# Small products on parts of TensorE's array, issued with the parts in turn

## The chip, the cores and the metric

The kernel runs on one core of one Trainium2 chip. The metric is device time in microseconds, the median of several runs. TensorE (PE) has two clock levels, 1.2 and 2.4 GHz; the profile gives the granted share of the full clock.

## What is computed

The reference is two blocks of a network on 256 tokens of width 2048, all in f32. The first has 16 meta tokens ahead of the sequence and mixes attention with a state space layer; the second mixes three branches, two of which are recurrences with a state of 128 x 128 for each head. What the change touches, cut from the reference:

```python
# block 1, state space: 64 groups of 16 channels, each with a complex state of 64
_, states = lax.associative_scan(_ssm_combine, (a, bu), axis=0)
y = jnp.real(jnp.einsum('lbgp,ghp->lbgh', states, c_c))          # the read-out
# block 1, attention: window of 128 plus 16 meta tokens, 16 heads of 64, 4 key heads
out = (jnp.einsum('bnkgqs,bnskd->bnqkgd', p_band, v_band)
       + jnp.einsum('bnkgqm,bmkd->bnqkgd', p_meta, v_meta))
```

In block 2 the delta rule needs the inverses of unit triangular matrices of 128 x 128 (one for each head, chunk and direction), and the gated linear attention needs the scores of pairs of tokens under products of gates, for 8 heads, 2 chunks of 128 tokens and 2 directions.

## The kernel before

**The weight stream.** `load_w` (L320) brings 128 x 1024 pieces of weights from DRAM, ACT rounds each to the high part (L328) and DVE subtracts to get the low part (L329). `linear` (L337) and `linear_t` (L373) multiply the parts with the activations' parts, three fp32r products for each pair of tiles (L349 to L351, L384 to L386). These products carry the lowest priority (`band(2)`), the loads `band(0)`, everything else `band(1)`. The order of each engine's queue is fixed when the kernel is built: a list scheduler takes, by priority, what it expects to be ready; the stream's products fill PE wherever a chain of `band(1)` waits. On the chip each engine then works its queue in that order.

**State space read-out.** `ssm_tile` (L592) handles one of 8 channel tiles with 4 state tiles. For a state tile, PE makes the input (L622), DVE rotates, scans (L630) and multiplies the state by cosines and sines into two tiles, and four f32 products of 128 rows, 32 columns and 256 moving columns add up in 32 partitions of `yps` (L635). These 32 partitions are one of four column parts of the array. After the fourth state tile DVE adds the skip term into `gel` (L636). The state and its products share one tag with five buffers (L273).

**Attention.** `attend` (L763) takes one key head and 128 queries at a time. At the end, for each half of the heads, two or three groups of tokens (16 meta tokens, 128, and for the second queries another 128) are multiplied with the probabilities; a half writes 64 of the 128 partitions of `o` (L814). The normalised keys lie in three tiles of 4 x 192 columns a token tile (`kp`, L668), written by one operation of DVE in `head_norm` (L661).

**Merge of blocks.** `merge_blocks` (L1150) puts inverses of 32 x 32 blocks together to 64 and to 128. For a pair of blocks it takes three stages (L1168, L1170, L1172), each of 8 small products into one PSUM tile and one eviction by ACT (L1174, L1176, L1178). The block pairs (`lo`, direction `d`, group of heads `g`) lie on different rows and columns of the array. It runs twice for the context (4 heads each) and once for all 8 heads.

**Scores.** In `gla_x`, for a head, a chunk and a direction, three products make the upper levels (L1497, L1504); then for each of four blocks of 32 tokens, six f32 products of 128 rows, 32 columns and 32 moving columns go to the 32 partitions of that block (L1509, L1510).

An f32 product shows in the trace as two matmul records, an fp32r product as one.

Of the kernel before, what the change touches and what calls it, by code (L numbers as in the profile page):

```python
# [53 lines left out]
def layout(inp):  # L54
# [42 lines left out]
    # block 2  # L97
# [40 lines left out]
    # constants of the shapes  # L138
# [18 lines left out]
    up = (i_[:, None] <= i_[None, :]).astype(np.float32)          # [s, t]: s <= t  # L157
# [13 lines left out]
    # segment sums [j, level, t]  # L171
# [9 lines left out]
    # transform at the 256 frequencies (f + 1/2) / 512; f and 255 - f share the sums over the even tokens (2 m)  # L181
    # and over the odd ones (2 m + 1): [m, (cos even, sin even, cos odd, sin odd), f], and the inverse [f, .., m]
# [18 lines left out]
# ----------------------------------------------------------------------------  # L201
# device side
# ----------------------------------------------------------------------------
def emit(tc, I, out, vat, cat):
# [29 lines left out]
    @contextmanager  # L234
    def behind(*ins):
        """activations of the block queue behind the given ones: the tables of their functions change once"""
        with ExitStack() as es:
            for i in ins:
                es.enter_context(tc.issue_after(i.ins))
            yield  # L240

    def dma(out_, in_):
        """transfer of a chain: ahead of the stream's"""
        with band(-1):
            nc.sync.dma_start(out_, in_)
# [27 lines left out]
    t_p = p2.enter_context(tc.tile_pool(name="t", bufs=5))  # L273
# [34 lines left out]
    side = [None, 0.0, 0.0]      # work that rides on the stream: generator, steps per load, steps due  # L308
# [11 lines left out]
    def load_w(ap):  # L320
        """ap: [128, 2048] in DRAM -> two halves of (hi, lo) parts"""
# [16 lines left out]
    def linear(xh, xl, W, ci, evict, toks=((0, 128), (128, 256)), kb0=0, nkb=None, mid=None):  # L338
        """token-major chunk of 512 columns: evict(t, psum)"""
# [12 lines left out]
        for kb in range(nkb):  # L352
            held = []
            for i, h, l in load_w(W[ci, kb0 + kb]):
                if kb < nkb - 1:
                    for t in range(len(toks)):
                        products(t, kb, i, h, l)
                else:
                    # the last weights: one token tile after the other, so that the first is evicted early
                    products(0, kb, i, h, l)  # L360
                    held.append((i, h, l))
# [11 lines left out]
    def linear_t(xh, xl, W, ci, n, evict, mid=None):  # L373
        """channel-major chunk of 256 columns (2 channel tiles) for n tokens: evict(j, psum)"""
# [18 lines left out]
    def split(src, hi, lo, scale=None):  # L393
        """hi + lo = src * scale, src in PSUM or SBUF"""
# [23 lines left out]
    def transpose_in(src, hi, lo, gcol, k, tag="a"):  # L418
        """src: list of (ap [p, D], p); one k tile into hi/lo [128, sum p]"""
# [8 lines left out]
    def ada_steps(p, row, dst, j0, n):  # L428
        """dst[:, j0 + j] = sum_k silu(c)[k] w_ada[k, (j0 + j) * 128 + p] + b_ada, for n column tiles"""
# [19 lines left out]
    def modulate_in(src, dst, sc, sh, k, ks=None):  # L449
        """k tile of the transposed src * sc + sh, split into dst"""  # L450
# [11 lines left out]
    # =====================================================================  # L462
    # block 1: norm, projections
    # =====================================================================
# [8 lines left out]
    p1.close()  # L473

# [18 lines left out]
    def poly(o, xx, coef):  # L493
        """o = sum coef[i] xx^i, highest last"""
# [5 lines left out]
    def exp_parts(a, nm_):  # L500
        """returns p2 = 2^n and q = expm1(r) with a = n ln2 + r"""
# [31 lines left out]
    # reduced angle  # L533
# [17 lines left out]
    # lambda_bar - 1 = em1 - 2 e sn^2 + 2 i e sn cs  # L551
# [21 lines left out]
    def rotation(s):  # L573
        """cosine, sine and negated sine of the state tile's angles over the tokens"""
# [16 lines left out]
    def ssm_tile(c, u):  # L591
        """u: [128 channels, L1] in SBUF; channel tile c -> gel[c]"""  # L592
# [21 lines left out]
        yps = psum("sm", [128, NT])  # L614
        for j in range(4):
            s = 4 * c + j
# [14 lines left out]
            pc, ps_ = (tl(t_p, [128, 2, L1], "t")[:, :, 0:NT] for _ in range(2))  # L631
            tt(pc, z[:, :, 16:], cos2[:, :, 16:], ALU.mult)
            tt(ps_, z[:, :, 16:], sin[:, 0:1, 16:].to_broadcast([128, 2, NT]), ALU.mult)
            for i, (pr, w) in enumerate(((pc[:, 0], Cr), (pc[:, 1], nCi), (ps_[:, 0], nCi), (ps_[:, 1], nCr))):
                T.matmul(yps[32 * j:32 * j + 32, :], w[:, j], pr, start=(i == 0), stop=(i == 3))  # L635
# [18 lines left out]
    def head_norm(ps, p, nh, dst):  # L654
        """ps [p, nh*64] -> dst [p, nh, 64] normalised (without gain)"""
# [6 lines left out]
        V.tensor_tensor(out=dst, in0=ps.rearrange("p (h d) -> p h d", d=64),  # L662
                        in1=s_[:p, :nh].unsqueeze(2).to_broadcast([p, nh, 64]), op=ALU.mult)

    kp = [tl(at_p, [128 if t < 2 else 16, 4, 192], f"kp{t}") for t in range(3)]
    vv = [tl(at_p, [128, 256], f"vv{t}") for t in range(3)]
    for t in range(3):
        nc.gpsimd.memset(kp[t], 0.0)  # L668
# [3 lines left out]
    def ev_kv(t, ps):  # L672
        p = 16 if t == 2 else 128
        head_norm(ps[:, 0:256], p, 4, kp[t][:p, :, 64:128])
# [3 lines left out]
    def turn_k():  # L678
        for v in range(4):
            for h in range(2):  # L680
                with band(0):
                    ps = psum("a", [128, L1])
                    for t, (lo, hi) in enumerate(toks3):
                        p = hi - lo
                        T.transpose(ps[:, lo:hi], kp[t][:p, v, 64 - 64 * h:192 - 64 * h], ident[:p, :p])
# [20 lines left out]
    # =====================================================================  # L706
    # block 2: modulation of the context, its state projections
    # =====================================================================
# [66 lines left out]
    def attend(v, t):  # L775
# [35 lines left out]
        for half in range(2):  # L811
            for i, (lo, hi, tv) in enumerate(groups):
                p = hi - lo
# [15 lines left out]
    def chan_norm(src, goff, gname):  # L829
        """rmsnorm over 8 channel tiles [128, NT]; into mixT[goff:]"""  # L830
# [55 lines left out]
    def turn_h(c):  # L886
        """the 4 k tiles of x's chunk c, times the gain of the norm"""
# [23 lines left out]
    def mlp(xT, Wu, Wd, evd, scale=None, mid=None, after=None):  # L911
        """evd(c, g): eviction of a chunk; scale: row [128, NT] of factors of the tokens before the activation;
        mid: work after the first half of the first product; after(c): after the last group's chunks"""
# [40 lines left out]
    grow = scratch("grow", [2, D])  # L954

    # lower bounds
# [9 lines left out]
    def gla_gates(xs, hb, nh):  # L966
        """xs: per direction (d, lf, kk, sm), tiles [128 dk, nh, NT] with the forget logits in kk:
        log forget into lf, key into kk"""
# [3 lines left out]
        for d, lf, kk, sm in xs:  # L972
# [4 lines left out]
            # the two factors of max(f, 1e-30), each in the range of Ln  # L977
# [13 lines left out]
    def excl_scan(o, g, rev, n):  # L991
        """o[t] = sum of g over j > t (rev) or j < t, over the last axis"""
# [45 lines left out]
    def conv_silu(p, o, src, r0, wname, wcol, row):  # L1038
        """o: short convolution along the tokens (rows of `row` tokens) and silu of src[r0:r0+128] (DRAM)"""
# [11 lines left out]
    def l2n(p, pk, xs, scales):  # L1051
        """each of xs [128, NT]: * scale / sqrt(sum over partitions x^2 + 1e-6), in place"""
# [17 lines left out]
    def delta_gates(p, pk, src):  # L1070
        """g, beta and exponentials of sums of g, tokens on partitions; kept in pk"""
# [8 lines left out]
        # log1p(e) = 2 atanh(e / (2 + e))  # L1080
# [20 lines left out]
        # exponentials of the sums: inclusive prefix, exclusive suffix, total; [128, kind, dir, c, h]  # L1101
# [13 lines left out]
    def block_inverse(p, MX, XT, KD):  # L1115
        """32x32 diagonal blocks of MX [128, 2 KD, 128] (unit triangular, diagonal not stored): the inverses
        go to MX, their transposes to XT [128, 2 KD, 64]"""
# [32 lines left out]
    def merge_blocks(p, MX, XT, KD):  # L1150
        pt = tl(p, [128, KD, 64], "T4c")
        for n, los in ((32, (0, 64)), (64, (0,))):
            work = [(lo, d, g) for lo in los for d in range(2) for g in range(KD // 8)]
            for stage in range(3):
                for lo, d, g in work:
                    one, two = slice(lo, lo + n), slice(lo + n, lo + 2 * n)
                    a, q = (one, two) if d == 0 else (two, one)
                    xc = slice(a.start % 64, a.start % 64 + n)
                    ks = slice(d * KD + g * 8, d * KD + g * 8 + 8)
                    # pt rows q: the block of direction d; both directions of one lo share its other half  # L1160
                    pg = pt[q, g * 8:g * 8 + 8, 0:n]
                    if stage == 2 and not (n == 32 and lo == 64 * d):
                        continue
                    ps = psum("sm" if d else "tp", [128, 8, n])
# [719 lines left out]
```

## Time and profile before

| | |
|---|---|
| runs | 3671.91, 3675.52, 3684.11 us; median 3675.52 |
| profiled execution | span 3676.8 us, from the first to the last instruction; the profile gives no other time for it |
| PE busy | 3504.3 us, 95% |
| DVE, ACT busy | 2609.8 us, 71%; 1882.7 us, 51% |
| DMA | 755.29 MB, 205 GB/s over the span |
| TensorE clock | mean granted share 0.979 |

Busy time is the time in which an engine has an instruction under way. Matmuls overlap one another, so what a product costs PE is read from the start of one record to the start of the next, not from its duration.

### The profile page before, as it was taken

The page shows a single profiled execution, that of the slowest core. Times are in us where ns is not written, and L with a number is a line of the kernel's source. Part 1 is how long each engine was busy: PE and PEld are TensorE (multiplying, and loading weights), DVE is VectorE, ACT ScalarE, POOL GpSimd, SP SyncE. Part 2 cuts the span into 40 slices and gives each one's busy share as a digit, 9 for nine tenths or more (in the row PEclk, how much of TensorE's full clock was granted, in tenths as well). Part 3 has the DMA queues.
Part 4 walks back from the last instruction along what each step waited for, and adds up shares of the span by engine and source line. Part 5 has one row for each costly group of instructions (what it writes and reads, how often), then busy time and mean ns, then how long its engine had stood idle before and what let it go on. Part 6 is the DMA issues. An engine that isn't in the chain of part 4 may idle for free.

```text
span 3676.8 us, 59387 instructions
## 1 busy us (share of the span) xinstructions
PE 3504.3 (95%) x23228; PEld 3027.8 (82%) x23228; DVE 2609.8 (71%) x4047; ACT 1882.7 (51%) x2945; POOL 2.3 (0%) x7
## 2 busy tenths in 40 slices
PE   6899999999999989989999999999999999999998
PEld 6568689887887869789888889877887798989897
DVE  8887777696968656666957578888865665555557
ACT  4466766544356434445536555645444454535353
POOL 0000000000000000000000000000000000000000
PEclk9999999999999999999989999999999999999999
DMA  8844346565667778776656864466556566666655
GB/s 290 272 160 130 118 162 191 178 205 176 212 205 250 247 246 257 244 257 220 203 181 207 291 203 149 155 202 197 166 182 196 192 216 223 212 225 217 214 191 174
DMA packets 272419, 755.29 MB, mean 205 GB/s; under 512 B 52301, under 2 KB 97525, under 8 KB 271093
## 3 DMA queue, kind: packets, MB, share of 16 engines
q1 hardware_dynamic: 272138, 751.49, 62.7%
q8 instruction: 182, 2.98, 0.3%
q14 instruction: 99, 0.81, 0.1%
HBM read 720.37 MB, written 31.01 MB: 204 GB/s over the span
## 4 chain that ended last, share of the span: by engine, by line
PE 57%; DMA 16%; DVE 10%; issue 4%; ACT 2%; SPq 0%; DVEq 0%; ACTq 0%
DMA w<-in_w_ada_dram 10%; PE ps L351 9%; PE ps L350 9%; PE ps L349 9%; PE ps L385 7%; PE ps L386 7%; PE ps L384 7%; DVE wl L329 4%; DVE w L439 1%; ACT wh L328 1%; PE ps L1509 1%; DVE T4c L488 1%; PE ps L635 1%; DMA w<-in_hy_w_dram 1%; PE ps L1170 1%
## 5 line engine op out<-in xcount | busy, mean ns | idle before, releaser
L328 ACT ACTIVATE wh<-w 128x1024 fp32r<-128x1024 f32 x1016 | 1074.1, 1058 | 1201.5 <-PE ps L351 533.1
L329 DVE TENSOR_TENSOR wl<-w,wh 128x1024 fp32r<-128x1024 f32 x1016 | 1236.6, 1220 | 577.0 <-ACT wh L328 571.7
L384 PE MATMUL ps<-Ah,wh 128*128 128x256 f32 (+1 forms) x3904 | 1116.0, 286 | 26.0 <-DVE r L491 16.4
L386 PE MATMUL ps<-Ah,wl 128*128 128x256 f32 (+1 forms) x3904 | 1119.4, 287 | 17.1 <-DVE wl L329 16.7
L385 PE MATMUL ps<-Al,wh 128*128 128x256 f32 (+1 forms) x3904 | 1118.4, 287 | 2.6 <-DVE Al L397 1.5
L384 PEld LDWEIGHTS ps<-Ah,wh 128*128 128x128 f32 x3904 | 747.3, 191 | 39.9 <-DVE r L491 20.0
L386 PEld LDWEIGHTS ps<-Ah,wl 128*128 128x128 f32 x3904 | 747.6, 192 | 32.3 <-DVE wl L329 22.7
L385 PEld LDWEIGHTS ps<-Al,wh 128*128 128x128 f32 x3904 | 744.0, 191 | 11.6 <-issue 6.8
L350 PE MATMUL ps<-wl,Bh 128*128 128x512 f32 x1344 | 534.4, 398 | 18.9 <-DVE wl L329 18.8
L351 PE MATMUL ps<-wh,Bl 128*128 128x512 f32 x1344 | 538.6, 401 | 0.0
L349 PE MATMUL ps<-wh,Bh 128*128 128x512 f32 x1344 | 534.4, 398 | 3.4 <-DVE r L491 2.3
L439 DVE SCALAR_TENSOR_TENSOR w<-w,cb 128x1024 f32<-128x1024 f32 x256 | 311.9, 1222 | 251.1 <-DMA w<-in_w_ada_dram 245.2
L350 PEld LDWEIGHTS ps<-wl,Bh 128*128 128x128 f32 x1344 | 254.9, 190 | 84.7 <-DVE wl L329 26.8
L349 PE MATMUL ps<-wh,Ah 128*128 128x512 f32 x752 | 298.6, 401 | 8.7 <-ACT wh L328 4.7
L350 PE MATMUL ps<-wl,Ah 128*128 128x512 f32 x752 | 302.6, 402 | 4.4 <-DVE wl L329 4.3
L349 PEld LDWEIGHTS ps<-wh,Bh 128*128 128x128 f32 x1344 | 255.5, 190 | 59.9 <-DVE r L491 3.6
L351 PE MATMUL ps<-wh,Al 128*128 128x512 f32 x752 | 300.2, 399 | 0.0
L351 PEld LDWEIGHTS ps<-wh,Bl 128*128 128x128 f32 x1344 | 254.7, 190 | 55.2 <-issue 1.4
L349 PEld LDWEIGHTS ps<-wh,Ah 128*128 128x128 f32 x752 | 139.9, 187 | 47.0 <-ACT wh L328 8.3
L350 PEld LDWEIGHTS ps<-wl,Ah 128*128 128x128 f32 x752 | 140.6, 187 | 41.6 <-DVE wl L329 7.9
L351 PEld LDWEIGHTS ps<-wh,Al 128*128 128x128 f32 x752 | 140.6, 187 | 34.9 <-issue 3.7
L923 ACT ACTIVATE r<-r 128x256 f32<-128x256 f32 x128 | 53.1, 417 | 92.0 <-DVE r L491 90.0
(566 smaller groups left out, 3424.9 us busy)
## 6 DMA issues: line engine op xcount, KB each, us to landing
w<-in_w_ff_dram SPq DMA_DIRECT2D x288, 512.0 KB, 4.7
w<-in_w_ada_dram SPq DMA_DIRECT2D x256, 512.0 KB, 4.8
w<-in_w_up_dram SPq DMA_DIRECT2D x128, 512.0 KB, 4.9
w<-in_w_down_dram SPq DMA_DIRECT2D x128, 512.0 KB, 4.9
w<-in_w_gate_dram SPq DMA_DIRECT2D x96, 512.0 KB, 4.5
w<-in_w_out_dram SPq DMA_DIRECT2D x64, 512.0 KB, 4.3
w<-in_w_hy_dram SPq DMA_DIRECT2D x48, 512.0 KB, 5.1
w<-in_w_br_dram SPq DMA_DIRECT2D x48, 512.0 KB, 4.6
```

Source lines behind the costliest of these rows:

```text
L328: A.activation(out=h, in_=w, func=AF.Copy)
L329: V.tensor_tensor(out=l, in0=w, in1=h.bitcast(F32), op=ALU.subtract)
L349: T.matmul(acc[t], xh[k][:, lo:hi], hs, start=(k == 0), stop=False)
L350: T.matmul(acc[t], xh[k][:, lo:hi], ls, start=False, stop=False)
L351: T.matmul(acc[t], xl[k][:, lo:hi], hs, start=False, stop=(k == nk - 1))
L384: T.matmul(acc[c], h[:, s], xh[k][:, 0:n], start=(k == 0), stop=False)
L385: T.matmul(acc[c], h[:, s], xl[k][:, 0:n], start=False, stop=False)
L386: T.matmul(acc[c], l[:, s], xh[k][:, 0:n], start=False, stop=(k == nk - 1))
L439: V.scalar_tensor_tensor(out=w, in0=w, scalar=1.0, in1=cb, op0=ALU.mult, op1=ALU.mult, accum_out=part[:, j, i:i + 1])
L488: V.tensor_tensor(out=o, in0=a, in1=b, op=op)
L635: T.matmul(yps[32 * j:32 * j + 32, :], w[:, j], pr, start=(i == 0), stop=(i == 3))
L923: A.activation(out=r, in_=r, func=AF.Square)
```

## The change

In four places the loops are turned so that neighbouring products in PE's queue use different parts of the array. Comments are gone as well.

1. `ssm_tile`: the four read-out products of a state tile are kept in a list; after every second state tile the products of both are issued, one of the first, one of the second, and so on. The products have tiles of their own (six buffers of 2 x 256 columns); the state keeps three. Both pools are opened after the first phase's tiles are given back.
2. `attend`: the loop over groups of tokens is now outside, the loop over halves inside.
3. `merge_blocks`: in a stage and a group of heads, all block pairs get their PSUM tile first; then product 0 of each, product 1 of each, up to 7; then their evictions.
4. `gla_x`: the six kinds of products are the outer loop, the four blocks the inner.

To make room for the buffers of 1, the keys move into eight tiles of the pool of activations; the key norm writes them by four operations of DVE, and they are cleared by nine instructions on GpSimd in place of three.

```diff
-    t_p = p2.enter_context(tc.tile_pool(name="t", bufs=5))
...
     p1.close()
+    t_p = p2.enter_context(tc.tile_pool(name="t", bufs=3))
+    pr_p = p2.enter_context(tc.tile_pool(name="pr", bufs=6))
...
         yps = psum("sm", [128, NT])
+        terms = []
         for j in range(4):
+            terms.append([])
...
-            pc, ps_ = (tl(t_p, [128, 2, L1], "t")[:, :, 0:NT] for _ in range(2))
+            pc, ps_ = (tl(pr_p, [128, 2, NT], "pr") for _ in range(2))
             tt(pc, z[:, :, 16:], cos2[:, :, 16:], ALU.mult)
             tt(ps_, z[:, :, 16:], sin[:, 0:1, 16:].to_broadcast([128, 2, NT]), ALU.mult)
             for i, (pr, w) in enumerate(((pc[:, 0], Cr), (pc[:, 1], nCi), (ps_[:, 0], nCi), (ps_[:, 1], nCr))):
-                T.matmul(yps[32 * j:32 * j + 32, :], w[:, j], pr, start=(i == 0), stop=(i == 3))
+                terms[-1].append((w[:, j], pr))
+            if j % 2:
+                for i in range(4):
+                    for jj in (j - 1, j):
+                        w, pr = terms[jj][i]
+                        T.matmul(yps[32 * jj:32 * jj + 32, :], w, pr, start=(i == 0), stop=(i == 3))
...
-        V.tensor_tensor(out=dst, in0=ps.rearrange("p (h d) -> p h d", d=64),
-                        in1=s_[:p, :nh].unsqueeze(2).to_broadcast([p, nh, 64]), op=ALU.mult)
+        if isinstance(dst, list):
+            for h in range(nh):
+                V.tensor_scalar(out=dst[h], in0=ps[:, h * 64:(h + 1) * 64], scalar1=s_[:p, h:h + 1], scalar2=None,
+                                op0=ALU.mult)
+        else:
+            V.tensor_tensor(out=dst, in0=ps.rearrange("p (h d) -> p h d", d=64),
+                            in1=s_[:p, :nh].unsqueeze(2).to_broadcast([p, nh, 64]), op=ALU.mult)
...
-    kp = [tl(at_p, [128 if t < 2 else 16, 4, 192], f"kp{t}") for t in range(3)]
+    kp = [[tl(act_p, [128, 192], f"Bh{8 + 4 * t + v}") for v in range(4)] for t in range(2)]
+    kp_m = tl(at_p, [16, 4, 192], "kp2")
+    kp.append([kp_m[:, v] for v in range(4)])
...
-        for half in range(2):
-            for i, (lo, hi, tv) in enumerate(groups):
-                p = hi - lo
+        for i, (lo, hi, tv) in enumerate(groups):
+            p = hi - lo
+            for half in range(2):
                 T.matmul(o[64 * half:64 * half + 64], vv[tv][:p, v * 64:(v + 1) * 64],
                          pts[i][:p, half::2], start=(i == 0), stop=(i == len(groups) - 1))
...
-            work = [(lo, d, g) for lo in los for d in range(2) for g in range(KD // 8)]
             for stage in range(3):
-                for lo, d, g in work:
+                for g in range(KD // 8):
+                    work = []
+                    for lo in los:
+                        for d in range(2):
+                            if stage == 2 and not (n == 32 and lo == 64 * d):
+                                continue
...
+                            work.append((a, q, xc, ks, pt[q, g * 8:g * 8 + 8, 0:n],
+                                         psum("sm" if d else "tp", [128, 8, n])))
                     for i in range(8):
-                        k = ks.start + i
+                        for a, q, xc, ks, pg, ps in work:
+                            k = ks.start + i
+                            if stage == 0:
+                                T.matmul(ps[q, i], MX[a, k, q], XT[a, k, xc], start=True, stop=True)
+                            elif stage == 1:
+                                T.matmul(ps[a, i], pg[:, i], MX[q, k, q], start=True, stop=True)
+                            else:
+                                T.matmul(ps[q, i], MX[q, k, q], pg[:, i], start=True, stop=True)
+                    for a, q, xc, ks, pg, ps in work:
...
-                    for b in range(4):
-                        s_ = slice(32 * b, 32 * b + 32)
-                        g_ = slice(t * 128 + 32 * b, t * 128 + 32 * b + 32)
-                        for i in range(5):
-                            T.matmul(cf[s_, i * 32:(i + 1) * 32], E[:, 2 + i, s_], qE[:, 2 + i, s_], start=True, stop=True)
-                        T.matmul(cf[s_, 160:192], kk[:, g_], q[:, g_], start=True, stop=True)
+                    for i in range(6):
+                        for b in range(4):
+                            s_ = slice(32 * b, 32 * b + 32)
+                            g_ = slice(t * 128 + 32 * b, t * 128 + 32 * b + 32)
+                            l_, r_ = (E[:, 2 + i, s_], qE[:, 2 + i, s_]) if i < 5 else (kk[:, g_], q[:, g_])
+                            T.matmul(cf[s_, i * 32:(i + 1) * 32], l_, r_, start=True, stop=True)
```

## Rows read from the trace of the kernel before

**Rows 1.** Cores view (span, granted clock) and page part 1: busy us, share, instructions.

```profile
core 0: 3676.8 us, clock 0.979
...
PE 3504.3 (95%) x23228; PEld 3027.8 (82%) x23228; DVE 2609.8 (71%) x4047; ACT 1882.7 (51%) x2945; POOL 2.3 (0%) x7
```

**Rows 2.** Page part 4: the chain that ended last, by engine.

```profile
PE 57%; DMA 16%; DVE 10%; issue 4%; ACT 2%; SPq 0%; DVEq 0%; ACTq 0%
```

**Rows 3.** Windows: length, busy us of each engine, granted clock, DMA share, GB/s.

```profile
200.00:530.00 330.00, 323.27 (x1847) 239.41 (x1848) 255.93 (x443) 230.59 (x450) 0.00 (x0) 0.98 0.41 134
1902.40:1926.30 23.90, 23.45 (x286) 22.25 (x283) 3.01 (x5) 9.79 (x21) 0.00 (x0) 0.50 0.35 126
2149.30:2351.80 202.50, 201.84 (x2788) 184.52 (x2786) 172.47 (x348) 115.63 (x324) 0.00 (x0) 1.00 0.44 143
```

**Rows 4.** Waits of DVE and ACT, 200 to 530: total us, times, longest.

```profile
DVE wl L329 <- ACT wh L328: 29.6, 27, 2.2
DVE g L491 <- PE ps L635: 12.9, 7, 4.3
...
ACT wh L328 <- PE ps L385: 36.7, 23, 3.1
```

**Rows 5.** Timeline of PE, a read-out: start, us, what, records.

```profile
317.77 1.05 PE L635 MATMUL ps<-t,nC 128*32 128x256 f32 x4
318.75 0.39 PE L384 MATMUL ps<-Ah,wh 128*128 128x256 f32 x1
```

**Rows 6.** Timeline of PE, two calls of attention's last products.

```profile
306.99 0.64 PE L814 MATMUL ps<-pt,vv 16*64 16x256 f32 x2
307.56 0.38 PE L384 MATMUL ps<-Ah,wh 128*128 128x256 f32 x1
307.87 1.79 PE L814 MATMUL ps<-pt,vv 128*64 128x256 f32 x6
309.59 0.50 PE L782 MATMUL ps<-Bl,Bh 128*128 128x272 f32 x1
...
350.80 3.23 PE L814 MATMUL ps<-pt,vv 16*64 16x256 f32 x12
353.96 0.50 PE L622 MATMUL ps<-Bl,lB 128*128 128x272 f32 x1
```

**Rows 7.** Timeline of PE, two merges; ACT's evictions of the second (lines view).

```profile
839.55 0.59 PE L1168 MATMUL ps<-XT,MX 32*32 32x32 f32 x13
...
852.28 1.22 PE L349 MATMUL ps<-wh,Bh 128*128 128x512 f32 x2
...
1896.73 1.19 PE L1168 MATMUL ps<-XT,MX 32*32 32x32 f32 x32
1897.88 2.34 PE L1170 MATMUL ps<-MX,T4c 32*32 32x32 f32 x64
...
1922.04 0.79 PE L1260 MATMUL ps<-T4a,Bh 128*128 128x256 f32 x1
...
L1174 ACT ACTIVATE T4c<-ps 32x256 f32<-32x256 f32 (+1 forms) x12 | 5.2, 444 | 12.9 <-PE ps L1168 12.6
```

**Rows 8.** Timeline of PE, one block of scores and what follows.

```profile
2155.99 0.33 PE L1497 MATMUL ps<-qE,E 128*64 128x64 f32 x2
...
2156.32 0.48 PE L1509 MATMUL ps<-qE,E 128*32 128x32 f32 x11
2156.60 0.20 PE L1510 MATMUL ps<-g,Bh 128*32 128x32 f32 x1
2156.63 0.20 PE L1509 MATMUL ps<-qE,E 128*32 128x32 f32 x1
2156.64 0.20 PE L1510 MATMUL ps<-g,Bh 128*32 128x32 f32 x1
2156.66 0.41 PE L1509 MATMUL ps<-qE,E 128*32 128x32 f32 x9
...
2157.60 0.49 PE L1522 MATMUL ps<-S,qP 128*128 128x128 f32 x2
```

**Rows 9.** Lines of DVE, 200 to 530: busy, mean ns.

```profile
L488 DVE TENSOR_TENSOR bt<-bcw,si 128x128 f32<-128x128 f32 x12 | 3.4, 286 | 0.2
```

More of the change, by code (lines that the diff above doesn't have):

```diff
@@ L661, in head_norm @@
         rstd_of(s_[:p, :nh], 64, 1e-6, p)
-        V.tensor_tensor(out=dst, in0=ps.rearrange("p (h d) -> p h d", d=64),
-                        in1=s_[:p, :nh].unsqueeze(2).to_broadcast([p, nh, 64]), op=ALU.mult)
-    kp = [tl(at_p, [128 if t < 2 else 16, 4, 192], f"kp{t}") for t in range(3)]
+        if isinstance(dst, list):
[8 more added lines that the diff above has]
+    kp.append([kp_m[:, v] for v in range(4)])
     vv = [tl(at_p, [128, 256], f"vv{t}") for t in range(3)]
-    for t in range(3):
-        nc.gpsimd.memset(kp[t], 0.0)
+    for k_ in (*kp[0], *kp[1], kp_m):
+        nc.gpsimd.memset(k_, 0.0)
     toks3 = ((16, 144), (144, 272), (0, 16))
@@ L673, in ev_kv @@
         p = 16 if t == 2 else 128
-        head_norm(ps[:, 0:256], p, 4, kp[t][:p, :, 64:128])
+        head_norm(ps[:, 0:256], p, 4, [k_[:p, 64:128] for k_ in kp[t]])
         A.activation(out=vv[t][:p], in_=ps[:, 256:512], func=AF.Copy)
@@ L684, in turn_k @@
                         p = hi - lo
-                        T.transpose(ps[:, lo:hi], kp[t][:p, v, 64 - 64 * h:192 - 64 * h], ident[:p, :p])
+                        T.transpose(ps[:, lo:hi], kp[t][v][:p, 64 - 64 * h:192 - 64 * h], ident[:p, :p])
                     A.activation(out=kT[v][h], in_=ps, func=AF.Copy)
@@ L1152, in merge_blocks @@
         for n, los in ((32, (0, 64)), (64, (0,))):
-            work = [(lo, d, g) for lo in los for d in range(2) for g in range(KD // 8)]
             for stage in range(3):
-                for lo, d, g in work:
[L1156 to L1164, printed above, removed]
-                    for i in range(8):
-                        k = ks.start + i
+                for g in range(KD // 8):
[4 more added lines that the diff above has]
+                                continue
+                            one, two = slice(lo, lo + n), slice(lo + n, lo + 2 * n)
+                            a, q = (one, two) if d == 0 else (two, one)
+                            xc = slice(a.start % 64, a.start % 64 + n)
+                            ks = slice(d * KD + g * 8, d * KD + g * 8 + 8)
+                            work.append((a, q, xc, ks, pt[q, g * 8:g * 8 + 8, 0:n],
+                                         psum("sm" if d else "tp", [128, 8, n])))
+                    for i in range(8):
+                        for a, q, xc, ks, pg, ps in work:
[7 more added lines that the diff above has]
+                    for a, q, xc, ks, pg, ps in work:
@@ L1167, in merge_blocks @@
                         if stage == 0:
-                            T.matmul(ps[q, i], MX[a, k, q], XT[a, k, xc], start=True, stop=True)
+                            A.activation(out=pg, in_=ps[q], func=AF.Copy)
                         elif stage == 1:
-                            T.matmul(ps[a, i], pg[:, i], MX[q, k, q], start=True, stop=True)
+                            A.activation(out=MX[a, ks, q], in_=ps[a], func=AF.Copy, scale=-1.0)
                         else:
-                            T.matmul(ps[q, i], MX[q, k, q], pg[:, i], start=True, stop=True)
@@ L1173, in merge_blocks @@
-                    if stage == 0:
-                        A.activation(out=pg, in_=ps[q], func=AF.Copy)
-                    elif stage == 1:
-                        A.activation(out=MX[a, ks, q], in_=ps[a], func=AF.Copy, scale=-1.0)
-                    else:
-                        A.activation(out=XT[q, ks, xc], in_=ps[q], func=AF.Copy, scale=-1.0)
+                            A.activation(out=XT[q, ks, xc], in_=ps[q], func=AF.Copy, scale=-1.0)
     def delta_heads(p, pk, src, h0, nh, gates, row, S_in, S_out, tb):
```

## Prediction

> **What bounds the kernel now.** I read the busy shares first: the span is 3676.8 us at a mean granted clock of 0.979, and PE is busy 95% of it [rows 1]. A busy PE can still be a waiting PE, so the chain of waits comes next: 57% of it is PE, 16% DMA, 10% DVE [rows 2]. Then the stretches where the edited products run [rows 3]. From 200 to 530 us (read-out and attention) PE is busy 323.3 of 330 us, DVE 255.9. From 1902.4 to 1926.3 (the longest merge of blocks and what follows it) PE is busy 23.5 of 23.9 us at a granted clock of 0.50, DVE 3.0. From 2149.3 to 2351.8 (scores of the gated linear attention) PE is busy 201.8 of 202.5 us, DVE 172.5. All three are PE stretches. The waits say the same: in the first, DVE's longest waits are for ACT's copy of the weights, 29.6 us, and for the read-out products, 12.9 us, and ACT's own longest wait is for PE to let go of weight buffers, 36.7 us [rows 4]. So a microsecond taken from PE's queue there is a microsecond of the kernel, until DVE fills up. The sum is made against the span of the profiled execution; it lies 1.3 us above the median of the runs (3675.52), which I neglect.
>
> **How a part-array product shows.** Each f32 product leaves two matmul records. Records on the same part follow each other; records on different parts can run side by side. The last products of one 32-column part and the first of the next show it: L1510 at 2156.60 and .64, L1509 at .63 and .66 [rows 8], so each keeps a step of 0.03 to 0.04 us while the other does too, 15 to 20 ns a record, while 32 records on one part take from 1896.73 to 1897.88, 36 ns each [rows 7]. So two parts in turn cost half. Whether four parts cost a quarter, and whether the same holds for 256 moving columns, no row shows.
>
> **(a) State space read-out (L635).** 8 channel tiles of 4 state tiles have 4 products each: 128 products, 256 records. They come in groups of two products: 4 records from 317.77 to the next other start at 318.75, 0.98 us [rows 5]. 64 groups of 0.98 are 63 us, all but a few in PE-bound time. In the new order two state tiles alternate. Their products add into one PSUM tile, and products into one PSUM tile stay in program order: at 306.99 the first half's 16-row product is followed by a product of the stream, not by the second half's 16-row product, which needed nothing more [rows 6]. So I expect the pair in three pieces: the first product of tile j-1 alone as soon as its cosine product is there (two records, 0.57 us as at 306.99 to 307.56 [rows 6]); then (j), (j-1), (j), (j-1) when tile j has its first term: four records on each of two parts, 0.98; then the last three, again at most 0.98. 2.53 us against 4 x 0.98 = 3.92, 1.4 us for each of 16 pairs: 22 us. If the halves come as two full alternating groups it is 3.92 - 1.96, 31 us; if 256-column records of two parts don't overlap it is nothing. I take 22, since the overlap at 32 columns is the nearest row. The last tile's DVE add (the 12.9 us wait) follows the last product in either order.
>
> **(b) Attention times values (L814).** With two groups of tokens it takes 306.99 to 307.56 and 307.87 to 309.59, 2.29 us; with three, 350.80 to 353.96, 3.16 us [rows 6]; four calls of each, 21.8 us. The two halves write 64 columns each and now alternate product by product: half, 10.9 us; at the other end nothing. I take 10.
>
> **(c) Merge of blocks (L1168 to L1172).** 896 records. The largest merge, 416 records without a break, lasts from 1896.73 to 1922.04, 25.3 us, and most of it at the low clock of 1.2 GHz [rows 3, 7]; one context half has 208 records in 839.55 to 852.28, 12.7 us [rows 7]; with the other half and the pieces ahead the sum is 51 us. The new loop issues up to four chains in turn. But each has a PSUM tile of its own, so order is set by when each is ready: at 1896.73 32 records of one chain run by themselves because the others' blocks have not landed, and from stage to stage each chain waits for its own eviction on ACT, 0.44 us each, 12 of them in the largest merge [rows 7]. So I count two chains at a time for half of the products: a quarter of 51, 13 us, plus 2 us for less time at the low clock. Ends: all four chains abreast and full clock, 36 us; or lockstep, PE standing behind four evictions of 0.44 us at each of 20 stages (five in each of the two context halves, and five for both groups of heads of the last merge), 35 us, less 15 to 20 regained: a loss of 15 to 20. Stream products usually fill such holes, so I take +15.
>
> **(d) Scores (L1509, now one loop).** 32 blocks (8 heads, 2 steps, 2 directions) of 1.61 us, 2155.99 to 2157.60 [rows 8]. The 48 records from 2156.32 on take 1.28 us, 27 ns each. With the four column parts in turn at the step seen for two, 16 ns, 0.77: 0.51 us a block, 16 us. Four truly abreast would be 0.36, 29 us; no overlap beyond today's, nothing. I take 16.
> The Trainium skill weighs against (d): "TensorE: Matmul & The Clock Gate", in its section on the gap of 56 ns, puts a floor of some 25 ns between starts of matmuls however few their columns. The trace has 15 to 20 over four records [rows 8], and the row decides; by the page 48 records would take 1.2 us and (d) would give 3 us.
>
> **(e) Costs added.** The key norm on DVE becomes four operations of 64 columns where there was one, three times; with a 128-column operation at 0.29 us [rows 9] that is at most 12 x 0.29 less the 3 it replaces, no shorter, 2.6 us, ahead of the queries' projection whose accumulators wait for it; at the other end it is hidden. I take 2. Nine clears on POOL instead of three have no predecessor and lie under the first projection. The buffers for the state (3 of z and its partner, 6 of the products) suffice for a pair: four products are held, two are free for the next tile, and DVE works through one tile at a time. The keys now lie in buffers that attention's outputs reuse much later. No DMA is added or moved.
>
> **Sum.** 22 + 10 + 15 + 16 - 2 = 61. What comes next as a bound is DVE in 200 to 530: it needs 255.9 of then 298 us, 86%, and in the scores 172.5 of 186, 93%. Serial chains rarely run that full, so I give back 2 us of the first and 4 of the second. 55 us net: 3676.8 - 55 = 3622.
>
> **Rivals.**
> 1. DVE takes over. With (a) and (b) worth 40% and (d) 45% of their sizes: 13 + 7 + 15 - 2 = 33 us, 3644. For it: DVE's 85% in the scores [rows 3]. Against: its waits there and in the read-out end with PE [rows 4].
> 2. More overlap: (a) 31, (b) 11, (c) 25, (d) 27, less 2 and the same 6: 86, 3591. For it: nothing in the rows caps overlap at two. Against: four abreast isn't seen.
> 3. The change doesn't do what it says: parts that share their rows do not run side by side with 256 columns, so (a) and (b) give nothing and (d) little: 15 + 3 - 2 = 16, 3661. Against it: the four starts within 0.06 us are column parts of the same 128 rows [rows 8]. For it: they are short.
> A rule of the skill says so more strictly: "TensorE: Matmul & The Clock Gate", Part 3, The mechanism, lets a weight load overlap products under way only where the row groups differ. The trace disagrees for 32 columns by the same rows.
> 4. Slower: the clock. In the merge PE was busy throughout and the granted clock still was 0.50 [rows 3]; the scores kept 1.00 with 52 of 202 us in small products. If their blocks, shortened and followed by waits for DVE, bring the clock down, each microsecond at 1.2 GHz costs half a microsecond of full-clock work. It decides from 110 us at the low clock, where the 55 are gone; if half of the scores' 186 us of work ran at the low level it would take 93 us more, 3715. Against it: the stream's full-array products still fill every gap there.
>
> **How the numbers follow.** Forecast 0.50 (own range 3607 to 3634), rival 1 0.17, rival 2 0.14, rival 3 0.11, rival 4 0.08. From 3580 to 3656 leaves out rivals 3 and 4 and little of rival 2: 0.8. A measurement of this kernel can tell 0.3%, 11 us, from no change: faster takes the forecast, rivals 1 and 2 and half of rival 3, 0.86; within 0.3% half of rival 3, 0.06; slower 0.08.
>
> **What would show it.** (a) right: read-out records of two parts starting a few ns apart and some 0.12 us a record; wrong: 0.25 us a record as now. (b) 1.1 to 1.6 us a call. (c) the merge from 1896 under 18 us; if lockstep, PE waits for ACT's evictions of L1174 to L1178. (d) blocks of 1.0 to 1.1 us; with four abreast 0.7. PE's busy total should fall by 45 to 75 us. The prediction is wrong if PE's total falls so far and the span does not: then waits for DVE in 200 to 530 or 2149 to 2350 take its place; or if the clock's mean falls below 0.979.

## The result, and the profile after

The changed kernel takes 3630.26 us (median of 4 runs, 3624.57 to 3634.63), the kernel before beside it 3677.26 (4 runs): ratio 0.986, 95% interval 0.9841 to 0.9878, which is 45 to 58 us less (the medians lie 47 us apart; the ratio on record is not their quotient, which would be 0.987). The forecast was 3622, with a range of its own from 3607 to 3634. The profiled execution has a span of 3632.9 us, 44 less than that of before; the rows below are from it.

Cores and busy shares, then the chain that ended last, of the changed kernel:

```profile
core 0: 3632.9 us, clock 0.978
...
PE 3452.0 (95%) x23228; PEld 2990.6 (82%) x23228; DVE 2610.2 (72%) x4056; ACT 1873.9 (52%) x2938; POOL 2.6 (0%) x13
...
PE 54%; DMA 15%; DVE 8%; issue 5%; ACT 3%; SPq 0%; DVEq 0%; ACTq 0%
```

PE does the same 23228 matmul records in 52 us less; DVE has what it had [rows 1]. The chain is still PE's by more than half, a little less than before [rows 2].

Windows of the changed kernel (length, busy time of each engine with instructions, granted clock, DMA share, GB/s): read-out and attention, the largest merge with its two stretches, the scores.

```profile
200.00:503.00 303.00, 294.95 (x1874) 231.41 (x1872) 256.66 (x444) 219.82 (x434) 0.00 (x0) 0.99 0.45 147
1877.03:1882.83 5.80, 5.08 (x145) 4.57 (x144) 0.00 (x0) 2.99 (x8) 0.00 (x0) 0.97 0.91 201
1882.83:1899.95 17.12, 17.12 (x290) 16.87 (x288) 1.23 (x2) 7.44 (x17) 0.00 (x0) 0.51 0.50 189
2129.50:2319.60 190.10, 185.55 (x2814) 165.31 (x2814) 174.83 (x354) 119.83 (x334) 0.00 (x0) 1.00 0.51 159
```

The first stretch has DVE's 256 us of before in 27 us less. The merge's longer part is still at 0.51 with PE busy all of it. In the scores PE, which had no idle time worth naming [rows 3], now has 4.6 us of it, and DVE stands at 174.8 of 190.1.

Waits of DVE and ACT, 200 to 503 (in all, times, longest):

```profile
DVE wl L328 <- ACT wh L327: 15.9, 20, 1.9
DVE g L492 <- PE ps L644: 11.1, 6, 2.5
...
ACT wh L327 <- PE ps L384: 27.0, 20, 2.8
```

ACT waits 27.0 us for PE where it waited 36.7 [rows 4]: PE lets go of the weight buffers sooner.

Timeline of PE, a pair of state tiles, and the early single product of another:

```profile
288.82 0.40 PE L644 MATMUL ps<-pr,bcw 128*32 128x256 f32 x1 [0.43 <-DVE pr L489]
288.83 0.40 PE L644 MATMUL ps<-pr,nC 128*32 128x256 f32 x1
289.06 0.38 PE L644 MATMUL ps<-pr,bcw 128*32 128x256 f32 x1
289.07 0.81 PE L644 MATMUL ps<-pr,nC 128*32 128x256 f32 x5
289.81 0.39 PE L385 MATMUL ps<-Ah,wl 128*128 128x256 f32 x1
...
291.53 1.05 PE L644 MATMUL ps<-pr,nC 128*32 128x256 f32 x6
292.51 0.38 PE L383 MATMUL ps<-Ah,wh 128*128 128x256 f32 x1
...
306.70 0.62 PE L644 MATMUL ps<-pr,bcw 128*32 128x256 f32 x2
307.25 0.72 PE L798 MATMUL ps<-Bl,Bh 128*128 128x272 f32 x2
```

Two parts start 10 ns apart, and eight records take the 0.99 us that four took [rows 5]. Timeline of PE, attention times values with two and with three groups of tokens:

```profile
304.88 1.23 PE L830 MATMUL ps<-pt,vv 16*64 16x256 f32 x8
306.04 0.72 PE L798 MATMUL ps<-Bl,Bh 128*128 128x272 f32 x2
...
345.33 1.66 PE L830 MATMUL ps<-pt,vv 16*64 16x256 f32 x12
346.92 1.19 PE L625 MATMUL ps<-Bl,lB 128*128 128x272 f32 x4
```

1.16 and 1.59 us for 2.29 and 3.16 [rows 6]. Timeline of PE, the long runs of the largest merge:

```profile
1877.03 1.75 PE L1188 MATMUL ps<-XT,MX 32*32 32x32 f32 x45
...
1882.83 6.02 PE L1188 MATMUL ps<-XT,MX 64*64 64x64 f32 x92
...
1893.22 3.56 PE L1188 MATMUL ps<-XT,MX 64*64 64x64 f32 x31
...
1896.64 3.38 PE L1190 MATMUL ps<-MX,T4c 64*64 64x64 f32 x63
1899.95 0.70 PE L1281 MATMUL ps<-T4a,Bh 128*128 128x256 f32 x2
```

From 1877.03 to 1899.95 there are 22.9 us where there were 25.3 [rows 7]. The first run has 35 ns a record (1877.03 to 1878.59 for 45), as one chain had before: the chains still come one after another. The row of 92 holds 32 records of 64 rows and 60 of 32 rows, and only its end alternates. Of the 64-row runs only the last, 63 records in 3.3 us, shows two parts in turn: 53 ns a record for 105 in the run of 31 ahead of it. Timeline of PE, a block of scores:

```profile
2142.16 0.33 PE L1518 MATMUL ps<-qE,E 128*64 128x64 f32 x2 [0.68 <-DVE S L492]
2142.42 0.22 PE L1525 MATMUL ps<-qE,E 128*32 128x32 f32 x2
2142.44 0.23 PE L1531 MATMUL ps<-qE,E 128*32 128x32 f32 x2
2142.47 0.20 PE L1525 MATMUL ps<-qE,E 128*32 128x32 f32 x2
2142.49 0.46 PE L1531 MATMUL ps<-qE,E 128*32 128x32 f32 x30
2143.01 0.49 PE L1544 MATMUL ps<-Bl,at 128*128 128x128 f32 x2
2143.43 0.27 PE L1531 MATMUL ps<-qE,E 128*32 128x32 f32 x8
2143.51 0.25 PE L1531 MATMUL ps<-g,Bh 128*32 128x32 f32 x8
2143.69 0.49 PE L1543 MATMUL ps<-S,qP 128*128 128x128 f32 x2
```

Eight records from 2143.43 to 2143.51, 10 ns each, where the long loop of before had 27 [rows 8].

**Where the time came from.** For the lines of each edited place (in the scores with the upper levels, which stand among them) I add up, over the timeline, the time from a block's first record to the next start of another line (us of PE, before and after): read-out 66.1 and 40.6, values 22.1 and 11.3, merges 50.9 and 49.4, scores 52.6 and 28.7: 61.7 less. Of it the span has 44 in this pair of executions. By the starts of the same products in both traces, 25.9 us are gained when attention ends (528.9 and 503.0) and 28.9 when the first merge begins (836.2 and 807.3). The stretch of the scores up to the last product behind them is 14.7 shorter (204.8 and 190.1); from the first score product to the last it is 19.4 shorter (202.4 and 183.0), and the rest lies behind them, where PE stands 2.05 us idle for ACT and works through more of the stream. Against that the dense stage from the second merge to the third, where behind that merge no line is edited, took 883.6 us at a clock of 0.97; before, 874.0 at 0.98. Single executions differ there by that much: the four kernels with one part each took 882.0 to 886.8 us (values alone, scores alone) or 873.8 to 875.0 (read-out alone, merges alone), and behind the second merge PE's queue holds the same 5239 records in the same order in all six. The lower clock level was granted for 54.6 us of the stage in the changed kernel and for 37.5 before; at half the speed the difference is worth an estimated 8.5 us, most of the 9.6. That is why parts are weighed below by their own stretches and by medians, not by the difference of two spans.

### The profile page after: what moved, and what is told of

The parts are those of the page before. It is cut to its first block, busy times and chain, and to the rows that moved or that the text cites. A ratio compares the mean times of both kernels' runs of the same rounds, so it can differ in the third digit from the quotient of the medians.

```text
span 3632.9 us, 59413 instructions
## 1 busy us (share of the span) xinstructions
PE 3452.0 (95%) x23228; PEld 2990.6 (82%) x23228; DVE 2610.2 (72%) x4056; ACT 1873.9 (52%) x2938; POOL 2.6 (0%) x13
## 4 chain that ended last, share of the span: by engine, by line
PE 54%; DMA 15%; DVE 8%; issue 5%; ACT 3%; SPq 0%; DVEq 0%; ACTq 0%
DMA w<-in_w_ada_dram 10%; PE ps L350 9%; PE ps L349 9%; PE ps L348 9%; PE ps L383 6%; PE ps L384 6%; PE ps L385 6%; DVE wl L328 4%; ACT wh L327 1%; DVE T4c L489 1%; DVE w L438 1%; PE ps L1188 1%; DVE T4a L1151 1%; PE ps L1190 0%; DMA w<-in_w_hi_dram 0%
## 5 line engine op out<-in xcount | busy, mean ns | idle before, releaser
L383 PE MATMUL ps<-Ah,wh 128*128 128x256 f32 (+1 forms) x3904 | 1117.9, 287 | 31.3 <-DVE r L492 19.4
L349 PE MATMUL ps<-wl,Bh 128*128 128x512 f32 x1344 | 536.0, 399 | 17.1 <-DVE wl L328 17.0
L350 PEld LDWEIGHTS ps<-wh,Bl 128*128 128x128 f32 x1344 | 255.1, 190 | 54.3 <-issue 1.0
L348 PEld LDWEIGHTS ps<-wh,Ah 128*128 128x128 f32 x752 | 140.6, 188 | 46.2 <-ACT wh L327 11.9
```

Source lines behind the costliest of these rows:

```text
L348: T.matmul(acc[t], xh[k][:, lo:hi], hs, start=(k == 0), stop=False)
L349: T.matmul(acc[t], xh[k][:, lo:hi], ls, start=False, stop=False)
L350: T.matmul(acc[t], xl[k][:, lo:hi], hs, start=False, stop=(k == nk - 1))
L383: T.matmul(acc[c], h[:, s], xh[k][:, 0:n], start=(k == 0), stop=False)
```

## The experiments

Theory A: in all four places PE sets the pace, so the time follows the PE time taken away. Rivals: another engine eats part of it; and for the merges, that order can't help at all.

**Each part alone, in the kernel before.** Four kernels, timed together (before 3682.28, 23 runs). The first holds the pairs of state tiles, with the buffers that they need and so the keys' normalisation; the others have one loop each in the new order.

```
 # read-out alone
...
-                T.matmul(yps[32 * j:32 * j + 32, :], w[:, j], pr, start=(i == 0), stop=(i == 3))
+            if j % 2:
+                for i in range(4):
+                    for jj in (j - 1, j):
...
 # values alone
-        for half in range(2):
-            for i, (lo, hi, tv) in enumerate(groups):
+        for i, (lo, hi, tv) in enumerate(groups):
+            for half in range(2):
...
 # merges alone
...
+                    for i in range(8):
+                        for a, q, xc, ks, pg, ps in work:
...
 # scores alone
-                    for b in range(4):
+                    for i in range(6):
+                        for b in range(4):
...
```

> The kernel before with the read-out in pairs alone (its buffers and the keys' new place with it); attention, merge and scores as before. Theory A (what an edit takes from TensorE's time comes off the span): the read-out's records fell from 66 to 41 us of TensorE time, so 25 us less, 2 of them given back by the key norm: 23 us off, about 3653. Rival (VectorE fills up in this stage): not more than 15 us off, with VectorE's waits for TensorE gone from 200 to 500 us.

> The kernel before with only attention's last products in turn. Theory A: 22.1 to 11.3 us of TensorE time, so 11 us off, about 3666. Rival (hidden beside VectorE's chain): at most 4 us off.

> The kernel before with only the merge of blocks in turn. Theory A (the chains are ready one after another, so the queue still holds them one after another): 1 to 2 us of TensorE time, no difference in the time, -4 to +2 us. Rival (lockstep: TensorE stands behind four evictions at each stage): 10 us slower or more. Second rival (the products do alternate and the gain is lost elsewhere): matmul starts in the merges half as far apart as before.

> The kernel before with only the scores in turn. Theory A: 52.6 to 28.7 us of TensorE time, 24 us off, about 3653. Rival (VectorE is at 92% in this stage and takes over): 10 to 15 us off and the stage from the first to the last score shrinks by no more than that.

Measured: read-out 3660.81, ratio 0.9938 (0.9918 to 0.9958), 21.5 us less; values 3671.48, 0.9970 (0.9957 to 0.9982), 10.8 less; merges 3679.64, 0.9988 (0.9975 to 1.0), 2.6 less; scores 3662.88, 0.9942 (0.9924 to 0.996), 19.4 less. They add up to 54.3, inside the whole change's 45 to 58, so no loss from one part to another shows within these intervals. Read-out and values come out as Theory A says. The 2.6 of the merges are not clear of no change; they speak against lockstep, which would be 10 us slower. The new buffers of the read-out were not run without the new order; its PE time in this kernel is 40 us for 66. Scores alone, the window of the stretch:

```profile
2161.60:2347.40 185.80, 183.50 (x2804) 162.78 (x2804) 173.47 (x353) 118.18 (x334) 0.00 (x0) 1.00 0.50 156
```

185.8 us for 204.8: 19.0 of the 23.9 us of PE come off, with DVE at 93% of what is left, so the rival with 10 to 15 is wrong for this stretch. The merge alone has the same long runs as in the whole change:

```profile
1906.23 6.02 PE L1172 MATMUL ps<-XT,MX 64*64 64x64 f32 x92
```

**The later tile first.** The changed kernel with one line altered.

```
-                    for jj in (j - 1, j):
+                    for jj in (j, j - 1):
```

> The changed kernel, with one thing altered: within a pair of state tiles the later tile's product comes first in each turn, so no product of the earlier tile is issued alone while the later one is still being made. Theory A (the core's time follows the TensorE time in the state-space stage): each pair is now one block of eight records, 0.98 to 0.99 us, in place of a single product of 0.55 us, eight records and a last run of six; with three single products of 0.55 us saved in part per channel tile I expect TensorE's read-out time of the stage to go from 40.6 to about 32 us, and the time 6 to 10 us below the changed kernel's, ratio to the kernel before about 0.983. Rival: the early single products fill time in which TensorE waits for VectorE's products anyway, so the later start gives all of it back; then the time is within 3 us of the changed kernel's, or 2 to 5 us above it.

Measured: 3616.35, ratio to before 0.9824 (0.9808 to 0.984); the changed kernel in the same session 3622.04, 0.9842 (0.9821 to 0.9864). The single product is gone: 18 blocks of eight records at 0.99 us and 7 of sixteen (six at 1.85, one at 2.38), 31.3 us of PE for 39.8. The medians are 5.7 us apart, but the intervals overlap: that the planner keeps the order of products into one PSUM tile is confirmed, its worth in time isn't settled.

**All four tiles at once.**

```
-            if j % 2:
+            if j == 3:
-                    for jj in (j - 1, j):
+                    for jj in (3, 2, 1, 0):
```

with 8 buffers for products in place of 6 and 2 for the state and its partner in place of 3 (the expectation calls them the exponentials').

> The changed kernel, with the read-out once for all four state tiles of a channel tile, their four column parts in turn, the last tile first; two more buffers for the products, one fewer for the exponentials. If four parts of 256 columns run beside one another as two do, a channel tile's read-out is two blocks of 16 records at about 1.0 us each, 2.0 us in place of 4.7 to 5.0 us: TensorE's read-out time falls by about 22 us, and the time by 15 to 22 us under the changed kernel's, if TensorE sets the stage. If only two parts fit, 16 records take about 2 us, the read-out stays near 32 us, and the time is like that of the kernel with the later tile first. Rival: VectorE, 257 us busy in this stage of some 300 us, now has its products held until the fourth tile, and TensorE waits for it; then the gain in TensorE time doesn't come off the span, and the time is the changed kernel's or up to 10 us longer.

Measured: 3611.14, 0.9816 (0.9794 to 0.9838); 10.9 us under the changed kernel's median. Timeline of PE in this kernel, a whole channel tile:

```profile
284.90 0.64 PE L644 MATMUL ps<-pr,bcw 128*32 128x256 f32 x8 [0.60 <-DVE pr L489]
285.36 1.48 PE L644 MATMUL ps<-pr,nC 128*32 128x256 f32 x24
286.77 0.39 PE L384 MATMUL ps<-Al,wh 128*128 128x256 f32 x1
```

32 records in 1.87 us, 58 ns each, against 245 for one part [rows 5]: four parts of 256 columns run beside one another. PE's read-out time is 16.0 us, 23.8 less than the changed kernel's, but only some 11 come off. Waits of DVE in this kernel, 88 to 530:

```profile
...
DVE t L489 <- PE ps L625: 11.9, 4, 3.7
...
DVE sBre L489 <- DMA bcw<-in_ssm_bc_dram: 7.0, 5, 2.0
DVE g L492 <- PE ps L644: 3.6, 4, 1.4
```

The wait for the read-out (the last row) is 3.6 us where the changed kernel in the same session has 11.0, and the chain of DVE's next channel tile now waits for its input product and for a transfer: 11.9 and 7.0 us, where that kernel has 5.8 and no row of 1.2 us or more for the transfer. The windows of 88 to 563 us of this kernel and of that one:

```profile
88.00:563.00 475.00, 437.36 (x2873) 360.13 (x2872) 410.23 (x714) 332.43 (x622) 0.00 (x0) 0.97 0.57 187
88.00:563.00 475.00, 448.09 (x2761) 350.41 (x2762) 400.45 (x693) 315.31 (x600) 0.00 (x0) 0.99 0.55 182
```

PE idles 37.6 us of it for 26.9, so 10.7 of the 23.8 us came back as idle time. So here the rival is half right: PE alone no longer sets the end of the stage, and DVE's serial chain takes part; which of its waits costs how much was not tested.

**Merges in forced order.** Each merge product is made to follow the one that the loop writes before it, and the block pairs are taken in reverse.

```
-                        for a, q, xc, ks, pg, ps in work:
+                        for a, q, xc, ks, pg, ps in reversed(work):
...
+                            with behind(*([] if prev is None else [prev])):
+                                    prev = T.matmul(...)
```

> The changed kernel, with the merge products of the blocks of triangular inverses chained one behind the other in the order in which the loop writes them, so that chains of different parts alternate product by product and none is issued as soon as its own inputs are ready. If the order in which chains became ready is why the merge took 49.4 us of TensorE in place of 50.9, this order makes neighbouring products use different parts, and the merge's TensorE time falls to 25 to 35 us. Of that up to 15 us come off the span, less what each stage of merges waits for all four evictions before it starts. Rival: the wait for the slowest chain at each level costs as much as the alternation saves, about 12 levels of 1 us: then the TensorE time falls, and the time is within 5 us of the changed kernel's or above it. Second rival: the products alternate and still take 32 ns each; then the parts of this shape don't run side by side at all.

Measured: 3619.37, 0.983 (0.9812 to 0.9849), 2.7 us under the changed kernel. Timeline of PE in this kernel, in the largest merge:

```profile
1861.20 1.02 PE L1190 MATMUL ps<-XT,MX 32*32 32x32 f32 x66 [3.11 <-DMA XT<-invt]
...
1865.60 1.85 PE L1192 MATMUL ps<-MX,T4c 32*32 32x32 f32 x64 [0.77 <-ACT T4c L1197]
...
1881.11 2.65 PE L1190 MATMUL ps<-XT,MX 64*64 64x64 f32 x64
1883.60 0.29 PE L1192 MATMUL ps<-MX,T4c 64*64 64x64 f32 x2
```

66 records within 1.02 us, where the changed kernel has 45 in 1.56: the parts do run side by side, so the second rival is wrong, and the order was what held them. The windows of the merge and of its last levels here:

```profile
1861.20:1886.51 25.31, 18.86 (x468) 15.97 (x468) 6.05 (x7) 14.13 (x30) 0.00 (x0) 0.60 0.67 241
1881.11:1886.51 5.40, 5.32 (x130) 4.83 (x129) 0.00 (x0) 3.47 (x7) 0.00 (x0) 0.88 0.51 167
```

PE's merge time over the kernel is 37.2 us for 52.4 in the changed kernel of the same session (49.4 in its first profile). But from the record ahead of each block to the block 14.4 us pass in all, where 2.7 passed (2.4 in the first), 8.0 of them with PE idle, and inside the 37.2 PE idles another 6.5: it waits for blocks that have not landed (the 3.11 in the first row) and for evictions on ACT. Most of the gain became waits; the first rival holds.

**Forced order for 64-row blocks alone.** By shape the forced order had taken the 64-row products from 22.5 to 10.8 us, and left the 32-row ones, with their waits, at 26.3 for 26.9. Part of the first fall is the clock: in the largest merge these levels ran at 0.51 in the changed kernel and at 0.88 here (the windows above).

```
-                        for a, q, xc, ks, pg, ps in work:
+                        for a, q, xc, ks, pg, ps in (work if n == 32 else reversed(work)):
...
+                            with behind(*([] if prev is None or n == 32 else [prev])):
...
```

> The changed kernel, with the product-by-product order forced for the merges of 64-row blocks alone; those of 32-row blocks stay as the scheduler issues them. With all merges forced, the 64-row products fell from 23 to 11 us of TensorE (two chains) while the 32-row products stayed near 26 us and TensorE waited 14 us at entries. If that reading holds, this kernel keeps the 11 to 12 us of the 64-row products and loses almost none of the waits: merge TensorE time about 38 us with entries near 3 us, and the time 5 to 12 us below the changed kernel's. Rival: what TensorE gains in the merge it waits for later, since the next consumers need the last eviction of a level; then the time is within 3 us of the changed kernel's.

Measured beside the changed kernel again (3629.52, ratio 0.9835, 0.9817 to 0.9853): 3628.33, 0.9835 (0.9816 to 0.9854). The PE time fell as expected, 41.2 us for 52.2, with 3.7 in front of blocks for 2.7; the time did not move, so the rival holds. Of where it goes I know only a part. When the third merge begins this kernel is 2.7 us ahead of the changed one; from there on PE idles 3.6 us more up to the scores and 3.7 more in the convolution branch, but the planner also put other products into these stretches (89 and 36 records), so I can't tell what of it the forced order causes. This stays open.

**Four tiles with forced 64-row blocks.** Both edits together.

> Read-out after all four state tiles together with the forced order in the merges of 64-row blocks. If both gains come off TensorE's time independently: 11 us (measured for the four tiles beside the changed kernel) plus 5 to 12 us, so 3599 to 3608 us, ratio to the kernel before 0.977 to 0.980. Rival: only the four tiles count, 3611 us, ratio 0.981.

Measured: 3619.79, 0.9808 (0.9783 to 0.9832): the rival's 0.981. It is 9.7 us under the changed kernel of its session, as the four tiles alone were 10.9 under theirs. The kernel with four tiles is the quickest seen, together with this one.

**The changed kernel again**, for the two comparisons above.

> The changed kernel unaltered, beside the other three for comparison in the same session: 3630 us, ratio to the kernel before 0.986. If the mean clock of the untouched dense stage differs from that of its first profile, that stage's length differs by 8 to 13 us with no edit.

> The changed kernel unaltered, beside the other two: 3622 to 3630 us, ratio to the kernel before 0.984 to 0.986.

Its ratios, 0.9842 and 0.9835, lie about 0.002 under the first; the three intervals overlap. From the three ratios the change is worth 51, 58 and 61 us, from the medians 47, 59 and 58. The first of the two came out 8 us below what I expected, the second within it. The dense stage took 883.9 and 880.6 us, so the 8 to 13 that I held possible did not show between profiles of the changed kernel.

## Why the prediction was right, and which term was wrong

The forecast was a net of 55 us; the parts alone give 54.3, and the whole 47 to 59 by medians. The bound was right, but the sum is right in part by luck, because errors cancel: of 63 us of PE in (a) to (d), (c) was 13.5 too high, (d) 7.9, (a) 3.5 and (b) 0.8 too low, which makes the measured 61.7.

**What bounds it.** Right. Read-out and values together took 36.3 us less of PE, and their kernels gained 32.3; the scores took 23.9 less and gained 19.4. The give-back is 4.0 and 4.5 us, against the 2 and 4 that I allowed; in the scores of the whole change it shows as PE idle, 0.7 us before [rows 3] and 4.6 after.

**(a) Read-out, 22.** Measured 25.5 of PE and 21.5 of time. The pieces came out as forecast: 0.55, 0.99 and 0.98, 2.54 us a pair (40.6 over 16) for 2.53. The base was 66.1 where I counted 63. What I left open, whether 256 columns on two parts overlap, is answered by the starts at 288.82 and .83.

**(b) Values, 10.** 10.8 of both.

**(c) Merges, 15: the step that failed.** "I count two chains at a time for half of the products" was to give 13. The changed kernel has 1.5 us less of PE, and alone the edit gives 2.6 of time, with an interval that reaches no change; the merge took 22.9 us, not under 18. Single executions spread by more than the 1.5: PE's merge time is 50.9 to 54.7 us in the four kernels with the old loop and 49.4 to 52.4 in six with the new one, 2.1 apart in the mean. I had named the reason myself, that each chain has its own PSUM tile and goes when it is ready, and should have followed it to the end: the loop writes an order, the planner issues by readiness, and one chain's eight products are ready together. The runs of 45 and 92 records show it, and the forced order shows that nothing else kept the parts from alternating. The "2 us for less time at the low clock" did not fail with it: at the largest merge the stretch at the lower level is 23.9 us long before [rows 3] and 17.1 after. In the four kernels with the old loop it is 23.9 to 27.3, in the six with the new one 17.1 to 20.5. At half the clock 6.8 us less of it are worth an estimated 3.4, so this alone could be what the merges gained. The 12 evictions that I counted for the largest merge are those of its first stage; with 16 records a chain its 448 records make 28 chains, and as many evictions.

**(d) Scores, 16: too small.** 23.9 us of PE. It is nearer to four parts abreast, the end that I had at 29: 10 ns between starts, not the 16 that I took from two parts. A block takes 0.90 us (28.7 over 32), between the 1.0 to 1.1 forecast and the 0.7 for four abreast. The Trainium skill, "TensorE: Matmul & The Clock Gate", section "Wait — 56ns, not 53.3ns?", puts a floor of about 25 ns under the distance of two starts; by this trace it does not hold between parts of the array (eight records from 2143.43 to 2143.51, 10 ns each).

**(e) Key norm, 2.** Not seen apart. One operation of 64 columns took 0.27 us, nearly as much as one of 128 with 0.29 [rows 9]:

```profile
L673 DVE TENSOR_SCALAR Bh<-ps,hss x8: 262/270/278, 154.5 to 157.7; 128x64 f32<-128x64 f32 x8
```

**Rivals.** DVE did not take over in the change itself; it does so in part in the kernel with four tiles, which takes another 24 us of PE. More overlap was true of (d), not of (c). Parts that share their rows do run side by side at 256 columns. The Trainium skill, "TensorEngine Tiling (Array Packing)", section "Available Configurations", lists four parts of 128 rows by 32 columns; the trace agrees, with the 32 records of four such parts in 1.87 us. The clock stayed at 1.00 in the scores. One sign of being wrong came up all the same: the mean clock of the profiled execution is 0.978, below the 0.979 that I set. Executions of the kernel before lie between 0.975 and 0.981, so this sign was finer than the spread and tells nothing.

## What to carry to other kernels

Products on different parts of the array overlap only if they stand next to each other in the queue; a loop that alternates them does this where they are ready together or share one PSUM tile, and a planner that goes by readiness undoes it otherwise, so look at the starts in the trace, not at the loop. Forcing the order moved most of the cost into waits, and neither forced kernel was clearly faster than the changed one; where all inputs are there at once it could pay, which was not tested. Before the sum, ask of each term whether what it needs is ready at once.

## What the runs showed of the hardware

Four column parts of 256 f32 columns run abreast at 58 ns a record, as two do at 123 (eight in 0.99) and one at 245. Small products on four parts start 10 ns apart. PE's granted clock was 0.51, nearly all of it the lower level of 1.2 GHz, over 17.1 us in which PE was busy with small products without a break; in the kernel with all merges forced its last levels, with two parts in turn, ran at 0.88. But the whole of that merge, 25.3 us, had a mean of 0.60, an estimated 20 us at the lower level: the low stretch came earlier there and was no shorter (one execution each). And the dense stage, the same code in the kernel before and in those with read-out, values or scores alone, takes 873.8 to 886.8 us from one execution to the next: 13 us, more than the term for the values.
